# A two-layer hybrid decoder: attention units in the order diff, fox, diff, fox, each gate right behind its unit

## The chip, the cores and the metric

The kernel runs on one core of one Trainium2 chip. The metric is the device time of one execution in microseconds, taken as the median over several runs; the profile is of one such execution. A core has a matrix engine (TensorE, PE in the rows; its weight loads are the separate row PEld), VectorE (DVE), ScalarE (ACT), GpSimd (POOL) and SyncE (SP), which here only issues transfers. Each engine works through its own list of instructions in a fixed order and waits where an operand is not there yet.

## The reference

Two layers over 1040 tokens (16 meta tokens, 1024 of the sequence), width 1024. Each layer normalises h, multiplies it by one wide matrix `w_in`, and runs two kinds of attention on the parts: four **diff** heads (two softmaxes, the second subtracted with a weight, queries and keys turned by rope) and eight **fox** heads (one softmax each, with a running sum of forget gates added to the scores). Outputs are gated by silu(z), multiplied by `w_out` and added to h.

```
dq, dk, dv, dz, fq, fk, fv, fz, f_logit = split(u @ w_in)
p   = softmax(rope(q1) rope(k1)^T/8) - lam * softmax(rope(q2) rope(k2)^T/8)   # diff, causal
o_a = rms_norm(p @ dv, subln_g) * (1 - lambda_init)
cum = cumsum(log_sigmoid(f_logit + b_forget))
o_b = softmax(fq fk^T/8 + cum_q - cum_k) @ fv                                # fox, causal
h   = h + concat[o_a * silu(dz), o_b * silu(fz)] @ w_out
```

After the second layer comes a last RMSNorm; the meta tokens are dropped.

## The kernel before

A layer is cut into eight **units** of 128 columns: units 0 to 3 are the diff heads, units 4 to 7 hold two fox heads each. For a unit the kernel does

- `unit_proj`: k, q and v of the unit from `XTh`/`XTl` (the normalised input, transposed, as a rounded part and its rest). A product of fp32 quality is three matmuls: weights hi x input hi, weights lo x input hi, weights hi x input lo. One of k, q, v or z is 72 matmuls at L356. The weights come by DMA into `wraw` (SP) and are split on POOL into `whi` (L332) and `wlo` (L335). For diff units the key and query go through rope: the result is copied to `raw` (ACT), its halves are swapped by small transfers `sw<-raw` (SP), POOL multiplies by the sine table (L531), DVE by the cosine (L530) and adds (L532), and DVE makes the low parts (L538). Fox units have no rope.
- `attend`: scores into `pss` (L709 the high parts, L711 the low parts with the augmented rows), a masked minimum over them on DVE (L715) which also copies them to `E`, the exponential on ACT (L722), for diff one subtraction on DVE (L733), for fox a scaling on POOL (L739), transposes of `E` on PE (L884), their split by ACT (L792) and DVE (L793), and the products with V (L816 to L819).
- `sub_norm` for diff units and `unit_gate` (the z product and its multiplication into the output `OT`; the result goes to the DRAM buffers `ms`). With `from_dram` the gate first reads the ungated output back into `otl`.

`forget(l)` makes the running sum for the fox heads: the logits go out to the DRAM buffer `fx` and come back in another layout, ACT and DVE take the logarithm and a scan, one matmul with a triangular matrix (L483) carries sums across, and four small transfers write the results to the DRAM buffers `augq` and `augk`, from where each fox unit reads four rows into its low-part tiles `q2` and `k2` (the second operand of L711). `proj_v01` makes V of two units together with the forget logits, token by token.

In the loop of a layer, `unit_proj` of the next unit stands behind `attend` of the present one; in time the instructions of both are interleaved, because the builder's planner fixes each engine's order at build time. So while one unit's scores go through DVE, ACT and POOL, PE has the next unit's projection to do, and in the following a **step** means one unit's attention beside the next unit's projection. Before, a layer has three steps diff beside diff, one diff beside fox (unit 3), three fox beside fox and the last unit beside what is left. The gates of units 0, 1 and 2 stand behind their units, that of 3 behind unit 4, and those of 4 to 7 behind unit 7. After that come the transposed split of all gated outputs (L1088, L1089, from `mt<-ms`), and the product with `w_out` (L1109).

At the start, PE runs forty warm-up products (L970), then transposes the input, then projects k of unit 0. The four quarters of unit 0's k weights and of its q weights (`wroom`) are split on POOL.

## Time and profile before

| | |
|---|---|
| time, three runs | 1475.85 us median (1472.94 to 1477.03) |
| profiled execution | 1479.28 us; span in the trace 1477.5 us; mean granted clock 0.988 |
| PE busy / weight loads busy | 1425.7 us (96%) / 1353.0 us (92%) |
| DVE, ACT, POOL busy | 974.1, 696.1, 629.8 us (66%, 47%, 43%) |
| chain that ended last | PE 70%, DVE 5%, DMA 3%, ACT 2% of the span |

The table is read as follows: PE has work on hand nearly all the time, and the chain that ended last runs mostly through it; but its busy time counts pipelined matmuls by modelled ends, so the row of weight loads beside it, in which a stretch without work shows as a gap, is the stricter one. The other engines are busy half to two thirds of the span on average, and not evenly.

### The profile page before, as it was taken

Reading aid. Unit: us, or ns where it says so; the run is one execution under the profiler, and the core shown is the slowest. Engines: PE = TensorE matmul, PEld = TensorE weight load, DVE = VectorE, ACT = ScalarE, POOL = GpSimd, SP = SyncE. Lnnn points to the kernel's source line nnn. Section 1 sums busy time; section 2 is a strip of 40 time slices with the busy share of each in tenths; the row PEclk is TensorE's granted clock in tenths of the full one; section 3 lists DMA queues with packets and bytes.
Section 4 is the critical chain, followed back from the end, with each engine's and each line's share of the span. In section 5 each row is a group of like instructions: output and inputs, shape, how many; then the busy total and the mean of one; then the engine's idle time right before and its main releaser. Section 6 shows DMA issues by size and latency. Waiting matters only on the chain.

```text
span 1477.5 us, 26876 instructions
## 1 busy us (share of the span) xinstructions
PE 1425.7 (96%) x9302; PEld 1353.0 (92%) x9302; DVE 974.1 (66%) x2721; ACT 696.1 (47%) x1729; POOL 629.8 (43%) x1118
## 2 busy tenths in 40 slices
PE   6998989899999999999999999999999999999997
PEld 6997989799999999987889989899999999999886
DVE  6568776867665666574556587777867476755653
ACT  4336454445454555464223364545555365644511
POOL 4545454534244434555006345554424343445500
PEclk8999999999999999999999999999999999999999
DMA  8334321524043333465235142315322423244632
GB/s 195 75 52 63 56 64 33 76 25 98 23 88 63 63 68 43 120 206 105 86 118 126 27 62 49 71 44 72 57 51 64 90 38 80 62 98 105 221 114 86
DMA packets 112280, 119.64 MB, mean 81 GB/s; under 512 B 15440, under 2 KB 92880, under 8 KB 112144
## 3 DMA queue, kind: packets, MB, share of 16 engines
q1 hardware_dynamic: 106768, 105.14, 33.3%
q10 hardware_dynamic: 5376, 12.78, 3.5%
q8 instruction: 73, 1.20, 0.3%
q14 instruction: 63, 0.52, 0.1%
HBM read 70.92 MB, written 21.54 MB: 63 GB/s over the span
## 4 chain that ended last, share of the span: by engine, by line
PE 70%; DVE 5%; DMA 3%; ACT 2%; issue 1%; SPq 1%; POOL 1%; DVEq 0%; ACTq 0%
PE pj L356 33%; PE pss L1109 6%; PE pj L1109 5%; PE pt L884 3%; PE pss L709 3%; PE pss L711 3%; PE po L819 2%; PE po L818 2%; PE pj L436 2%; PE pt L1109 2%; DVE E L715 1%; SPq L144 1%; DMA wraw<-in_w_in_dram 1%; PE po L816 1%; DMA mt<-ms 1%
## 5 line engine op out<-in xcount | busy, mean ns | idle before, releaser
L356 PE MATMUL pj<-XTh,whi 128*128 128x346 f32 (+5 forms) x1392 | 452.6, 328 | 5.6 <-POOL whi L332 3.6
L356 PE MATMUL pj<-XTh,wlo 128*128 128x346 f32 (+5 forms) x1392 | 451.5, 325 | 5.9 <-POOL wlo L335 5.9
L356 PE MATMUL pj<-XTl,whi 128*128 128x346 f32 (+5 forms) x1392 | 451.3, 325 | 0.0
L356 PEld LDWEIGHTS pj<-XTh,whi 128*128 128x128 f32 x1392 | 262.8, 190 | 9.9 <-POOL whi L332 5.1
L356 PEld LDWEIGHTS pj<-XTh,wlo 128*128 128x128 f32 x1392 | 263.9, 190 | 7.7 <-POOL wlo L335 6.6
L715 DVE CUSTOM_DVE_ANT_0 E<-pss,cst 128x456 f32<-128x456 f32 (+6 forms) x384 | 211.8, 557 | 79.8 <-PE pss L711 61.9
L356 PEld LDWEIGHTS pj<-XTl,whi 128*128 128x128 f32 x1392 | 263.5, 190 | 0.9
L722 ACT ACTIVATE E<-E,cst 128x400 f32<-128x400 f32 (+2 forms) x192 | 172.4, 898 | 138.7 <-DVE cst L715 125.8
L335 POOL TENSOR_TENSOR wlo<-wraw,whi 128x256 fp32r<-128x256 f32 x232 | 181.8, 784 | 22.5 <-PE pj L356 7.6
L793 DVE TENSOR_TENSOR ptl<-pt,pth 128x512 fp32r<-128x512 f32 (+1 forms) x240 | 147.7, 633 | 41.5 <-ACT pth L792 36.4
L739 POOL TENSOR_SCALAR E<-E,cst 128x400 f32<-128x400 f32 (+2 forms) x96 | 84.5, 881 | 187.3 <-DVE cst L738 157.9
L709 PE MATMUL pss<-k,qa 128*128 128x400 f32 (+7 forms) x448 | 154.1, 347 | 9.3 <-DVE cst L715 7.2
L332 POOL TENSOR_SCALAR whi<-wraw 128x256 fp32r<-128x256 f32 x232 | 106.9, 461 | 110.6 <-DMA wraw<-in_w_in_dram 85.4
L792 ACT CAST pth<-pt 128x512 fp32r<-128x512 f32 (+1 forms) x240 | 123.7, 545 | 63.4 <-PE pt L900 29.7
L692 POOL TENSOR_SCALAR XTl<-ql 64x128 fp32r<-64x128 f32 x136 | 54.3, 401 | 185.2 <-PE pss L711 137.3
L709 PEld LDWEIGHTS pss<-k,qa 128*128 128x128 f32 x448 | 85.4, 191 | 17.5 <-DVE cst L715 14.0
L884 PE MATMUL pt<-cst,E 128*128 128x128 f32 x576 | 86.7, 274 | 4.2 <-DVE cst L715 2.9
L818 PE MATMUL po<-pth,V 128*128 128x256 f32 x320 | 84.2, 286 | 0.0
L819 PE MATMUL po<-ptl,V 128*128 128x256 f32 x320 | 83.1, 288 | 0.7 <-DVE ptl L793 0.5
L531 POOL TENSOR_TENSOR sw<-sw,sin 128x694 f32<-128x694 f32 (+5 forms) x32 | 53.2, 1666 | 55.5 <-DMA sw<-raw 42.8
L884 PEld LDWEIGHTS pt<-cst,E 128*128 128x128 f32 x576 | 68.0, 141 | 7.5 <-DVE cst L715 4.2
L711 PE MATMUL pss<-k,q 68*128 68x400 f32 (+6 forms) x224 | 72.2, 325 | 0.0
(301 smaller groups left out, 2971.0 us busy)
## 6 DMA issues: line engine op xcount, KB each, us to landing
wraw<-in_w_in_dram SPq DMA_DIRECT2D x248, 128.0 KB
hb<-in_x_dram SPq DMA_DIRECT2D x16, 512.0 KB
wor<-in_w_out_dram SPq DMA_DIRECT2D x64, 128.0 KB
ms<-OT SPq DMA_DIRECT2D x8, 520.0 KB
k<-k ACTq DMA_DIRECT2D x16, 260.0 KB
h<-hb SPq DMA_DIRECT2D x8, 512.0 KB
ms<-OT SPq DMA_DIRECT2D x8, 512.0 KB
hb<-h SPq DMA_DIRECT2D x8, 512.0 KB
```

The costliest lines, as they stand in the source:

```text
L335: nc.gpsimd.tensor_tensor(out=lo, in0=raw, in1=hi.bitcast(F32), op=ALU.subtract)
L356: nc.tensor.matmul(ps[:, :n], lhsT=w, rhs=xx[:, k, t0:t0 + n], start=(k == 0 and i == 0), stop=(k == KT - 1 and i == 2))
L709: nc.tensor.matmul(ps[:, :nn], lhsT=U.Qa[m][:, t:t + P], rhs=U.K1[m][:, c0:c0 + nn], start=True, stop=False)
L711: nc.tensor.matmul(ps[:, :nn], lhsT=low[m], rhs=U.Kb[m][:, c0:c0 + nn], start=False, stop=True)
L715: nc.vector.tensor_tensor_reduce(out=E[:, c0:c0 + n], in0=ps[:, :n], in1=k, scale=-1.0, scalar=s[:, c - 1:c] if CHN and c else -NEG, op0=A ...
L722: nc.scalar.activation(E[:, :W], E[:, :W], AF.Exp, scale=-1.0, bias=lo, accum_out=s[:, 4:5])
L792: nc.scalar.copy(hi, ps)
L793: nc.vector.tensor_tensor(out=lo, in0=ps, in1=hi.bitcast(F32), op=ALU.subtract)
L818: nc.tensor.matmul(o[:, :256], lhsT=U.V[:, kb, hd, :], rhs=hi, start=False, stop=False)
L819: nc.tensor.matmul(o[:, :256], lhsT=U.V[:, kb, hd, :], rhs=lo, start=False, stop=last)
L884: nc.tensor.transpose(ps[:, (2 * a + b) * P:(2 * a + b + 1) * P], PP[:, k0:k0 + P], ident)
L1109: nc.tensor.matmul(ps, lhsT=xx[:, k, m0:m0 + P], rhs=wo[k][w][:, c], start=(k == 0 and i == 0), stop=(k == KT - 1 and i == 2))
```

## The change

The units are taken in the order 0, 4, 1, 5, 2, 6, 3, 7, and every gate stands right behind its own unit, so that no gate reads its unit back from DRAM. Steps are then diff beside fox (four in a layer) and fox beside diff (three), and the last unit is again 7. Since unit 4 is now second, `forget(l)` is drained before its projection is, and `proj_v01` makes V of units 0 and 4. The rope tables get a tag of their own (two buffers; they shared the slots of `q2`), the buffers `ptl` go from four to three, unit 0's q weights are issued behind the k weights on POOL as well as on SP, and the warm-up has thirty products.

```diff
+ORD = (0, 4, 1, 5, 2, 6, 3, 7)
-PLB = 4
+PLB = 3
-WARM = 40
+WARM = 30
-Z_AT = {0: [0], 1: [1], 2: [2], 4: [3], 7: [4, 5, 6, 7]}
+Z_AT = {0: [0], 1: [1], 2: [2], 3: [3], 4: [4], 5: [5], 6: [6], 7: [7]}
...
-                col = unit_cols(u)[2]
+                col = unit_cols(ORD[u])[2]
...
-            for u in range(2):
-                x = ps[:, P * u:P * u + P]
-                nc.scalar.copy(Vs[u][:, b, 0, :], x)
-                nc.vector.tensor_tensor(out=Vs[u][:, b, 1, :], in0=x, in1=Vs[u][:, b, 0, :].bitcast(F32), op=ALU.subtract)
+            x = ps[:, 0:P]
+            nc.scalar.copy(Vs[0][:, b, 0, :], x)
+            nc.vector.tensor_tensor(out=Vs[0][:, b, 1, :], in0=x, in1=Vs[0][:, b, 0, :].bitcast(F32), op=ALU.subtract)
+            V, x = heads(Vs[1][:, b], "p a (c d) -> p (a c) d"), ps[:, P:2 * P].rearrange("p (m d) -> p m d", d=64)
+            nc.scalar.activation(V[:, 0::3, :], x, AF.Copy, scale=0.5)
+            nc.vector.scalar_tensor_tensor(out=V[:, 1:3, :], in0=x, scalar=0.5, in1=V[:, 0::3, :].bitcast(F32),
+                                           op0=ALU.mult, op1=ALU.subtract)
...
-    with tc.issue_after(last_of(SP)):
+    with tc.issue_after(last_of(SP)), tc.issue_after(last_of(POOL)):
         prefetch(0, "q")
     for l in range(DEPTH):
-        tabs = (q2t("cos", F32), q2t("sin", F32))
+        tabs = [big.tile([P, L], F32, name=nm, tag="tab", bufs=2) for nm in ("cos", "sin")]
...
-        for j in range(8):
+        for at, j in enumerate(ORD):
             run_late()
             drain(attend(units[j]))
             here = Z_AT.get(j, [])
-            if j < 7:
+            if j == 0:
+                drain(forget(l))
+            if at < 7:
                 if j >= 4 and j not in here:
                     dma(ms[j][:, tq:], units[j].OT[:, tq:])
-                drain(unit_proj(l, j + 1, units[j + 1], tabs))
-            if j == 0:
-                drain(forget(l))
+                drain(unit_proj(l, ORD[at + 1], units[ORD[at + 1]], tabs))
```

Line numbers of the changed kernel are higher by 2 near the top and by 13 to 15 from `proj_v01` on (L356 is L358 there, L483 L498, L711 L726).

The first place is PE around the triangular matmul of `forget` in layer 0. Before, scores of unit 1, a diff unit, follow it, which read neither `augq` nor `augk`:

```order
L779 MATMUL pt_1405<-XTl_97,sq_1402 128x1 x2
L483 MATMUL pt_1694<-cst_87 128x1
L709 MATMUL pss_1909<-k1_1410,qa1_1538 128x264
L711 MATMUL pss_1909<-k1_1410,XTl_97 128x264
L709 MATMUL pss_1968<-k0_1409,qa0_1537 128x256
```

Now, the low part of unit 4's scores (`q2`, `k2`, which hold the augmented rows) stands four rows behind it, and unit 1's k products (`pj_0_640`) stand behind that:

```order
L794 MATMUL pt_1396<-XTl_97,sq_1393 128x1 x2
L498 MATMUL pt_1424<-cst_87 128x1
L954 MATMUL pt_1685<-cst_87 128x16
L954 MATMUL pt_1688<-cst_87 128x128 x4
L954 MATMUL pt_1694<-cst_87 128x128 x4
L845 MATMUL pss_1812<-k2_1547,q2_1556 128x16
L726 MATMUL pss_1848<-k2_1547,q2_1556 128x400
L358 MATMUL pj_0_640_2466<-XTh_96,whi_2381 128x346
```

So only nine small transposes are left between the matmul that makes the sums and the first matmul that needs them back from DRAM. (In layer 1 there are, besides eight of these, 25 projection products in that place.)

The second place is SP's queue at the same point of the changed kernel, where writes to `augq` and `augk`, the reads of them, the store of unit 0's gated output and weights of the next projection stand in one line:

```order
L328 DMA wraw_2508<-in_w_in_dram 128x2x128
L328 DMA wraw_2514<-in_w_in_dram 128x2x128
L146 DMA augq_109<-cst_87 128x65 x2
L146 DMA augk_110<-cst_87 128x65 x2
L146 DMA q2_1556<-augq_109 4x1040
L146 DMA q2_1557<-ql_1555 64x1040
L146 DMA k2_1547<-augk_110 4x1040
L146 DMA k2_1550<-augk_110 4x1040
L146 DMA q2_1557<-augq_109 4x1040
L146 DMA ms0_101<-OT_954 128x1040
L328 DMA wraw_2520<-in_w_in_dram 128x2x128
```

Before, the first read of `augq` stands some two dozen transfers behind its write. The third place is POOL at the start of layer 0: before, two and two of the q splits (`wroom`) stood between the last quarters of unit 0's k weights:

```order
L332 TENSOR_SCALAR whi_197<-wraw4_180 128x256
L332 TENSOR_SCALAR wroom_346<-cst_87 128x256 x2
L335 TENSOR_TENSOR wlo_195<-wraw4_180,whi_193 128x256
L332 TENSOR_SCALAR wroom_346<-cst_87 128x256 x2
L335 TENSOR_TENSOR wlo_199<-wraw4_180,whi_197 128x256
L335 TENSOR_TENSOR wroom_346<-cst_87,wroom_346 128x256 x4
```

and now all of k's are ahead of q's:

```order
L334 TENSOR_SCALAR whi_187<-wraw4_170 128x256
L337 TENSOR_TENSOR wlo_185<-wraw4_170,whi_183 128x256
L337 TENSOR_TENSOR wlo_189<-wraw4_170,whi_187 128x256
L334 TENSOR_SCALAR wroom_336<-cst_87 128x256 x4
L337 TENSOR_TENSOR wroom_336<-cst_87,wroom_336 128x256 x4
```

The last two `wlo` of k no longer have q splits ahead of them.

## Rows read from the trace of the kernel before

**Rows 1.** Page, first part: span, and busy time by engine.

```profile
span 1477.5 us, 26876 instructions
PE 1425.7 (96%) x9302; PEld 1353.0 (92%) x9302; DVE 974.1 (66%) x2721; ACT 696.1 (47%) x1729; POOL 629.8 (43%) x1118
```

**Rows 2.** Windows, first score of a unit to the next's: layer 0 units 0–6, layer 1.

```profile
core 0: us, PE busy (x) PEld busy (x) DVE busy (x) ACT busy (x) POOL busy (x), PEclk, DMA share, GB/s
...
86.00:153.00 67.00, 61.70 (x395) 57.74 (x395) 50.93 (x138) 34.27 (x87) 34.83 (x60) 1.00 0.37 51
153.00:226.00 73.00, 68.66 (x461) 66.08 (x459) 57.40 (x161) 35.67 (x91) 36.14 (x62) 0.98 0.33 61
226.00:312.00 86.00, 78.56 (x510) 74.08 (x511) 59.72 (x161) 38.81 (x101) 38.30 (x66) 0.96 0.35 54
312.00:374.00 62.00, 61.79 (x423) 60.52 (x423) 46.56 (x146) 31.36 (x85) 24.94 (x53) 1.00 0.33 63
374.00:461.00 87.00, 87.00 (x610) 85.56 (x609) 52.03 (x161) 42.93 (x110) 36.41 (x72) 1.00 0.28 63
461.00:531.00 70.00, 69.94 (x489) 69.01 (x488) 45.00 (x139) 37.67 (x95) 30.18 (x59) 1.00 0.31 57
531.00:605.00 74.00, 73.69 (x519) 72.01 (x519) 45.20 (x141) 39.76 (x99) 32.57 (x65) 1.00 0.39 67
...
825.00:885.00 60.00, 56.73 (x363) 54.57 (x362) 47.28 (x128) 33.20 (x80) 30.22 (x51) 0.94 0.39 55
885.00:967.00 82.00, 78.40 (x532) 75.30 (x531) 60.22 (x161) 38.03 (x94) 39.05 (x65) 1.00 0.28 54
967.00:1039.00 72.00, 71.04 (x482) 68.69 (x481) 56.02 (x148) 35.12 (x86) 37.26 (x64) 1.00 0.39 61
1039.00:1097.00 58.00, 58.00 (x406) 57.47 (x405) 43.69 (x124) 30.69 (x78) 23.98 (x52) 1.00 0.35 67
1097.00:1175.00 78.00, 77.50 (x546) 76.45 (x545) 47.52 (x143) 38.41 (x95) 31.16 (x62) 1.00 0.28 64
1175.00:1239.00 64.00, 64.00 (x456) 63.32 (x454) 42.02 (x124) 36.34 (x85) 32.22 (x64) 1.00 0.35 64
1239.00:1299.00 60.00, 59.59 (x422) 58.27 (x420) 40.67 (x123) 35.66 (x84) 24.62 (x50) 1.00 0.34 67
```

**Rows 3.** Windows of 10 us inside unit 1 and unit 2 of layer 0.

```profile
180.00:190.00 10.00, 8.25 (x54) 7.20 (x53) 9.94 (x28) 3.92 (x9) 7.61 (x13) 1.00 0.57 107
230.00:240.00 10.00, 10.00 (x75) 9.96 (x74) 5.34 (x14) 4.32 (x10) 1.65 (x4) 1.00 0.00 0
```

**Rows 4.** Chain that ended last: projection matmuls back to back (start, duration).

```profile
1371.33 9.09 PE pj L356 x58
```

**Rows 5.** Line L532: duration in ns, min/median/max, first and last start, forms.

```profile
L532 DVE TENSOR_TENSOR raw<-raw,sw x32: 496/846/1637, 49.3 to 1016.2; 128x694 f32<-128x694 f32 x9, 128x346 f32<-128x346 f32 x9, 128x684 f32<-128x684 f32 x4, 128x340 f32<-128x340 f32 x4
```

**Rows 6.** Triangular matmul of the forget sums, and the writes of its results (lines).

```profile
L483 PE MATMUL pt<-cst x4: 250/250/250, 174.9 to 899.1; 128*128 128x1 f32 x4
L144 SPq DMA_DIRECT2D augq<-cst x4: 338/414/1238, 176.6 to 901.6; - x4
L144 SPq DMA_DIRECT2D augk<-cst x4: 319/418/424, 177.6 to 903.6; - x4
```

**Rows 7.** Chain that ended last: shortest and longest small transfer in it.

```profile
265.27 3.78 DMA sw<-raw
992.62 1.89 DMA sw<-raw
```

**Rows 8.** Timeline of POOL at the start, and PE's wait (idle before, releaser).

```profile
30.89 2.49 POOL L332 TENSOR_SCALAR wroom<-cst 128x256 fp32r<-128x256 f32 x2 [1.90 <-DMA cst<-in_w_in_dram]
33.34 1.70 POOL L335 TENSOR_TENSOR wlo<-wraw,whi 128x256 fp32r<-128x256 f32 x1
35.10 0.60 PE L356 MATMUL pj<-XTh,wlo 128*128 128x272 f32 x1 [5.04 <-POOL wlo L335]
```

**Rows 9.** Groups by line in 605 to 690 us, the end of layer 0.

```profile
L1089 DVE TENSOR_TENSOR XTl<-mt,XTh 128x400 fp32r<-128x400 f32 (+1 forms) x14 | 10.0, 739 | 4.7 <-ACT XTh L1088 4.6
```

More of the change, by code (lines that the diff above doesn't have):

```diff
@@ L19 @@
 DVE = mybir.EngineType.DVE
+POOL = mybir.EngineType.Pool
 AF = mybir.ActivationFunctionType
@@ L401, in load_v01, with heads @@
         return his, los
+    def heads(ap, how):
+        return ap.rearrange(how, d=64)
     def proj_v01(l, his, los):
@@ L419, in proj_v01 @@
         nc.vector.tensor_tensor(out=vm, in0=ps[0:NM, :NV], in1=vm, op=ALU.add)
-        for u in range(2):
-            Vm, x = Vms[u][:, 0, :], vm[:, P * u:P * u + P]
-            nc.gpsimd.memset(Vm.bitcast(F32), 0.0)
-            nc.scalar.copy(Vm[0:NM], x)
-            nc.scalar.copy(Vm[64:64 + NM], x)
-            nc.vector.tensor_tensor(out=Vm[32:32 + NM], in0=x, in1=Vm[0:NM].bitcast(F32), op=ALU.subtract)
+        nc.gpsimd.memset(Vms[0].bitcast(F32), 0.0)
+        nc.gpsimd.memset(Vms[1].bitcast(F32), 0.0)
+        Vm, x = Vms[0][:, 0, :], vm[:, 0:P]
+        nc.scalar.copy(Vm[0:NM], x)
+        nc.scalar.copy(Vm[64:64 + NM], x)
+        nc.vector.tensor_tensor(out=Vm[32:32 + NM], in0=x, in1=Vm[0:NM].bitcast(F32), op=ALU.subtract)
+        Vm, x = heads(Vms[1], "p a (c d) -> p (a c) d"), vm[:, P:2 * P].rearrange("p (m d) -> p m d", d=64)
+        for r in (slice(0, NM), slice(32, 32 + NM)):
+            nc.scalar.activation(Vm[r, 0::3, :], x, AF.Copy, scale=0.5)
+            nc.vector.scalar_tensor_tensor(out=Vm[r, 1:3, :], in0=x, scalar=0.5, in1=Vm[r, 0::3, :].bitcast(F32),
+                                           op0=ALU.mult, op1=ALU.subtract)
         fn = slot("fn").rearrange("p (h b) -> p h b", h=8)
@@ L437, in proj_v01 @@
                                      start=(k == 0 and i == 0), stop=(k == KT - 1 and i == 2))
-            for u in range(2):
-                x = ps[:, P * u:P * u + P]
-                nc.scalar.copy(Vs[u][:, b, 0, :], x)
-                nc.vector.tensor_tensor(out=Vs[u][:, b, 1, :], in0=x, in1=Vs[u][:, b, 0, :].bitcast(F32), op=ALU.subtract)
+            x = ps[:, 0:P]
[4 more added lines that the diff above has]
+            nc.vector.scalar_tensor_tensor(out=V[:, 1:3, :], in0=x, scalar=0.5, in1=V[:, 0::3, :].bitcast(F32),
+                                           op0=ALU.mult, op1=ALU.subtract)
             nc.vector.tensor_tensor(out=fn[:, :, b], in0=ps[:, 2 * P:NV], in1=bfb[:, l], op=ALU.add)
@@ L601, in unit_proj @@
                 U.Kb.append(k2[0:68])
-        if j == 1:
+        if j == ORD[1]:
             U.V, U.Vm = vpre[l]
```

## Prediction

> **What bounds the kernel now.** The first part of the page says PE is busy 96% of the span and its weight loads 92% [rows 1]. That is close to the end: the arithmetic on PE is the same after the change (it only loses ten warm-up products), so all a new order can win is what PE still loses. To find where it loses, I cut the span at the first score matmul of each unit and read each stretch from the table of windows. Busy PE is a modelled figure and hides gaps, so I take as lost what the weight loads leave of a stretch, PEld against its length [rows 2].
>
> The reader should see three kinds of step. Diff beside diff, three in each layer, loses 67.0 - 57.7 = 9.3, 6.9 and 11.9 us in layer 0, and 5.4, 6.7 and 3.3 in layer 1: 43.5 us. Diff beside fox, one in each layer, loses 1.5 and 0.5. Fox beside fox, three in each, loses 1.4, 1.0 and 2.0, then 1.6, 0.7 and 1.7: 8.4 in all. The sum is 53.9 us, and four fifths of it lie in diff beside diff.
>
> Why there? In those stretches DVE is busy for 69 to 79% of the time, in fox beside fox for 60 to 68% [rows 2]. That share alone doesn't decide: diff beside fox stands at 75% as well and loses next to nothing. The windows of 10 us show what does. From 180 to 190, inside unit 1, DVE is busy for 9.94 of 10 and the weight loads for 7.20; from 230 to 240 DVE is at 5.34 and the loads at 9.96 [rows 3]. PE loses where DVE is full for some 10 us on end, because PE's scores wait for a bank that DVE has yet to reduce. What fills it so is a diff unit's own scores and subtraction together with the rope of the next diff unit. So the kernel is bound by PE, and by DVE in bursts of six steps.
>
> **The change, part by part.**
>
> *The order of steps.* After, each layer has four steps diff beside fox and three fox beside diff. For the first kind I take the rows there are: 4 x 1.5 + 4 x 0.5 = 8 us. The second kind isn't in this trace: a fox unit's scores, which go through POOL's scaling and not DVE's subtraction, beside a diff unit's rope. It is bounded by its two parents: fox beside fox, mean 1.5 in layer 0 and 1.3 in layer 1, and diff beside diff, mean 9.4 and 5.1. I take 3 and 1.5 a step, 13.5 for six, nearer to fox beside fox, because the burst has lost the diff attention's half, while the rope stays. Together 21.5 against 53.9: **-32.4**. The bounds of the second kind move this by -5 and +30.
>
> *The wait for the forget sums.* This one is new. Before, nothing near reads `augq`; in the changed order of PE, unit 4's low-part score stands behind the triangular matmul with nine small transposes between them in layer 0. After that matmul comes, by the times of before, 1.7 us until the first write is issued (174.9 to 176.6); the `augk` writes start at 177.6 and two of them take 0.4 each on the queue, so all four are out 3.5 us behind it [rows 6]. A write must land, then a read is issued (0.5) and must land, and PE is in order: nothing behind the score can start, unit 1's k products included. The nearest rows for a small transfer that something waits for are `sw<-raw` on the chain, 1.89 at the shortest and 3.78 at the longest [rows 7]. In layer 0, with 1.1 us for the transposes as cover: 3.5 + 1.89 + 0.5 + 1.89 - 1.1 = 6.7 to 10.5 us. In layer 1 the 25 products in between, at 9.09/58 = 0.157 us each [rows 4], cover 3.9 more: 2.8 to 6.6. I take the middle: 8.4 + 4.5, **+12.9**.
>
> The Trainium skill, in "DMA: Bandwidth & Descriptors", section "Anatomy of one DMA — SWDGE (gpsimd) path", fits a constant of some 2.0 us to each transfer and puts most of it to the receipt of the last write, longest where the target is HBM, as it is for `augq`. The page is on transfers issued another way; with 2.0 for both, an estimate from that page, layer 0 would wait 6.9 and layer 1 3.0, and the sum would be 3 us lower.
>
> *What piles up behind it.* While PE waits, unit 1's projection isn't begun, and part of its products stood ahead of the wait. Unit 4's scores then have fewer products beside them, so they load DVE more densely than other steps of their kind. Bounds: nothing (DVE has emptied its queue in the wait), or as dense as a diff beside diff step, 9.4 - 3 = 6.4 and 5.1 - 1.5 = 3.6. I take half, **+5**.
>
> *Gates and the ends of layers.* Before, the gates of 4 to 7 run at the end of a layer, so three z products more, 72 x 0.157 = 11.3 us each, stand beside unit 7's attention and the split of the gated outputs. After, only unit 7's gate is left there. The gates' work isn't gone, it fills other steps; what is left at the end is the DVE work: unit 7's scores and fourteen splits at L1089, 10.0 us [rows 9], on a stretch of PE that is 23 to 34 us shorter. Bounds: 0, if the splits of earlier units are spread ahead, and +10 in layer 0 if they all stand in PE's way. I take half, 5, in layer 0 and 2 in layer 1, where the first units' gates stand further back: **+7**. The read-back of four units for each layer falls away; it lay on POOL and SP and I give it nothing, since its place is covered by the same three gates' products.
>
> *Start.* PE waits 5.04 us at 35.10 for the last `wlo` of unit 0's k; POOL had done q's splits in between, with a wait of 1.90 for their data and 2.49 of work [rows 8]. With k's four quarters first, `wlo` can end 1.90 + 2.49 = 4.4 us earlier. The q splits come behind it, and V's behind those, so the delay may come back at the V product (lower bound 0), or PE may lose none of the 5.04 any more (upper). I take **-4**.
>
> *Costed at nothing.* Ten warm-up products fewer: they run while PE waits for the first input. V of unit 4 in two strided operations for each block on ACT and DVE: it replaces unit 4's own evacuation of the same elements. `ptl` three deep: DVE's split and PE's use of it are a few hundred ns apart in all rows that I read; where it bites, it is part of the end of layer 0.
>
> *Sum.* -32.4 + 12.9 + 5 + 7 - 4 = **-11.5 us**. The profiled execution took 1479.28, so it would be 1467.8; it lies 3.4 above the median of the runs shown, so that 1475.85 becomes **1464.4**, say 1465.
>
> **The rivals.**
>
> *Fox beside diff loses as much as diff beside diff (slower).* DVE's rope addition shares the time with POOL's scaling of E, which diff attention lacks; L532 takes 846 ns at the median and up to 1637 [rows 5], so it can be stretched to twice, and it is with another engine on the same tiles that one expects this. Six steps then lose 3 x 9.4 + 3 x 5.1 = 43.5 instead of 13.5: +30, **1494**. It ends on the slower side (over 1480.3) when the six lose more than 13.5 + 11.5 + 4.4 = 29.4 together, 4.9 a step. Against it: fox beside fox has the same scaling, and diff beside fox at 75% of DVE lost 1 us.
>
> *The wait and the ends eat the gain (no change).* If the forget wait is at its upper bound (+4.2), the piled-up step too (+5), and layer 0's end (+5): -11.5 + 14 = +2.7, **1478**. SP's queue speaks for it: behind the reads stand the store of unit 0's gated output, which must wait for the gate, and behind it two quarters of unit 1's q weights, so that projection may start late as well. Against it, each is a bound.
>
> *More comes back than I think.* Fox beside diff at its lower bound (-5), nothing piled up (-5), ends of layers free (-7): -28, **1447**.
>
> That the change does nothing is excluded, since three quarters of the steps get another partner.
>
> **How the numbers follow.** Three runs of this kernel lie 0.28% apart, so about 0.3%, 4.4 us, can be told from no change: 1471.4 to 1480.3 is the same. My forecast, 1465 with a range of its own of 1456 to 1474 (the forget wait, the start and the ends each at one of their bounds): 0.47, of which 0.07 falls above 1471.4. No change by the wait and the ends: 0.17, of which 0.05 is slower. Fox beside diff as bad as diff beside diff, in whole or for the greater part: 0.17, of which 0.02 remains the same. More comes back: 0.19. Faster 0.40 + 0.19 = 0.59, same 0.07 + 0.12 + 0.02 = 0.21, slower 0.05 + 0.15 = 0.20. The range for 8 in 10 leaves out about a tenth at either end: from 1448 to 1486.
>
> **What would show it.** In the windows of the changed trace: steps diff beside fox should lose at most 2 us, fox beside diff 1 to 4; PE should wait once for the forget rows behind L498, 7 to 10 us in layer 0 and 3 to 7 in layer 1, released by a transfer into `q2` or `k2`; the wait at 35 us should be gone or down to 1; DVE should be full from the last unit's scores to the splits in layer 0. The prediction is wrong if fox beside diff loses over 5 us a step, if the forget wait is over 12 or missing, or if the steps' loss moves to another engine, for instance POOL, which has the weights to split and E to scale in each fox beside diff step.

## The result, and the profile after

The changed kernel takes 1499.89 us (median of 4 runs, 1498.22 to 1503.87) against 1476.44 for the kernel before, run beside it: a ratio of 1.0163, with an interval of 1.0137 to 1.0190. It is slower by 1.6%; 1465 had been forecast, in a range up to 1486. The profiled execution is the longest of the four, 1503.87.

The first part of the page after the change, beside [rows 1]:

```profile
span 1502.2 us, 26738 instructions
PE 1433.0 (95%) x9282; PEld 1358.3 (90%) x9282; DVE 963.0 (64%) x2725; ACT 701.6 (47%) x1729; POOL 617.3 (41%) x1116
```

The span is 24.7 us longer. The weight loads leave 143.9 us of it empty where they left 124.5. PE did no more work than before (twenty matmul records fewer), but what it did took 5.3 us more of load time. That goes with a lower clock (a mean of 0.980 granted, 0.988 before), not with work.

The table of windows of the changed kernel has the start, the seven steps of layer 0 and its end, then the steps and the end of layer 1 (columns as in [rows 2]; units in the order 0, 4, 1, 5, 2, 6, 3):

```profile
0.00:73.00 73.00, 54.77 (x368) 53.42 (x368) 48.55 (x97) 31.16 (x65) 40.38 (x63) 0.90 0.74 145
73.00:150.00 77.00, 75.73 (x516) 74.43 (x517) 44.59 (x154) 34.75 (x91) 23.05 (x52) 0.98 0.34 43
150.00:231.00 81.00, 67.33 (x404) 60.71 (x403) 50.21 (x153) 38.14 (x94) 34.14 (x58) 0.87 0.24 47
231.00:303.00 72.00, 71.73 (x494) 70.43 (x491) 48.24 (x143) 36.00 (x95) 28.07 (x62) 1.00 0.35 64
303.00:381.00 78.00, 76.69 (x525) 74.42 (x525) 50.48 (x149) 37.00 (x92) 43.25 (x72) 1.00 0.31 51
381.00:455.00 74.00, 73.41 (x503) 72.14 (x503) 51.58 (x149) 38.93 (x100) 28.17 (x61) 1.00 0.43 71
455.00:533.00 78.00, 77.58 (x533) 75.12 (x532) 51.79 (x151) 39.20 (x96) 45.07 (x73) 1.00 0.23 45
533.00:607.00 74.00, 73.20 (x503) 71.88 (x503) 50.75 (x147) 36.74 (x98) 30.34 (x65) 1.00 0.36 72
607.00:700.00 93.00, 85.34 (x538) 77.73 (x537) 63.92 (x180) 56.34 (x145) 41.74 (x72) 0.96 0.42 107
...
826.00:896.00 70.00, 68.78 (x476) 68.01 (x477) 45.95 (x147) 35.57 (x91) 20.21 (x47) 0.98 0.32 48
896.00:964.00 68.00, 61.31 (x411) 58.48 (x411) 45.11 (x128) 33.17 (x76) 35.91 (x56) 0.97 0.28 54
964.00:1038.00 74.00, 72.18 (x495) 70.73 (x493) 50.34 (x143) 37.19 (x92) 28.64 (x62) 1.00 0.34 66
1038.00:1115.00 77.00, 76.29 (x532) 74.90 (x531) 52.00 (x138) 37.72 (x88) 44.22 (x73) 1.00 0.27 47
1115.00:1187.00 72.00, 71.11 (x492) 70.40 (x491) 48.65 (x136) 36.68 (x91) 26.17 (x58) 1.00 0.40 74
1187.00:1264.00 77.00, 76.74 (x538) 75.67 (x537) 51.20 (x140) 38.99 (x91) 46.10 (x74) 1.00 0.20 41
1264.00:1333.00 69.00, 69.00 (x476) 68.48 (x476) 46.59 (x134) 34.32 (x86) 26.79 (x57) 1.00 0.40 85
1333.00:1425.00 92.00, 88.16 (x553) 80.96 (x552) 61.18 (x167) 55.11 (x135) 37.62 (x65) 0.96 0.31 99
```

Read length minus PEld, as in the prediction. Twelve of the fourteen steps lose little: diff beside fox 2.6, 1.6, 1.9 and 2.1 us in layer 0, then 2.0, 3.3, 1.6 and 0.5; fox beside diff 3.6 and 2.9, then 2.1 and 1.3. The two others are the second step of each layer, 81 - 60.7 = 20.3 and 9.5 us, with 403 and 411 matmuls where the other steps have 476 to 538. Look at their count before the waits: they are short of products. (The count alone doesn't decide: before, steps with 423 and 405 matmuls lost 1.5 and 0.5 us [rows 2].)

To compare kernels whose stretches lie elsewhere, and to take in the clock, I use a second count: each matmul of a trace is priced at 0.456 us for 1000 columns and 0.109 at least (full rate), and a stretch loses its length less that sum. The prices are from the kernel before, where a matmul of 128 columns is followed by the next after 0.109 us in the median, one of 346 after 0.159 and one of 512 after 0.234. The last stretch is counted to the last matmul. The sum is 1380.7 us for the kernel before and 1378.5 after. What is lost, in us:

```
                 start  L0 steps  L0 steps  L0    L1 steps  L1 steps  L1    sum
                        1-2       3-7       end   1-2       3-7       end
before           21.2   16.2      19.2      9.7   14.1       7.6       1.0   89.1
changed          25.0   30.5      11.3     16.9   14.7       8.2       9.2  115.9
```

The difference, 26.8 us, is 24.7 of span and 2.2 of warm-up that isn't there. Of it 14.3 lie in the first two steps of layer 0, 15.4 in the two ends and 3.8 at the start; the later steps of layer 0 give back 7.9, and layer 1's steps hardly changed.

### The profile page after: what moved, and what is told of

Read it like the earlier page. It is cut to its first block, busy times and chain, and to the rows that moved or that the text cites. A ratio compares the mean times of both kernels' runs of the same rounds, so it can differ in the third digit from the quotient of the medians.

```text
span 1502.2 us, 26738 instructions
## 1 busy us (share of the span) xinstructions
PE 1433.0 (95%) x9282; PEld 1358.3 (90%) x9282; DVE 963.0 (64%) x2725; ACT 701.6 (47%) x1729; POOL 617.3 (41%) x1116
## 4 chain that ended last, share of the span: by engine, by line
PE 78%; DMA 7%; DVE 7%; issue 3%; ACT 2%; SPq 2%; POOL 2%; DVEq 0%; ACTq 0%; POOLq 0%
PE pj L358 39%; PE pss L1124 6%; PE pj L1124 5%; PE pss L724 4%; PE pss L726 4%; PE pt L899 3%; DMA wraw<-in_w_in_dram 3%; PE pj L448 2%; PE po L834 2%; PE po L833 2%; DMA sw<-raw 2%; SPq L146 2%; PE pt L1124 1%; PE po L831 1%; PE po L829 1%
## 5 line engine op out<-in xcount | busy, mean ns | idle before, releaser
L358 PE MATMUL pj<-XTh,whi 128*128 128x346 f32 (+5 forms) x1392 | 455.0, 328 | 7.8 <-DVE OT L803 3.3
L358 PE MATMUL pj<-XTh,wlo 128*128 128x346 f32 (+5 forms) x1392 | 450.8, 325 | 1.4 <-POOL wlo L337 1.4
L358 PE MATMUL pj<-XTl,whi 128*128 128x346 f32 (+5 forms) x1392 | 449.3, 324 | 0.0
L358 PEld LDWEIGHTS pj<-XTh,whi 128*128 128x128 f32 x1392 | 263.2, 189 | 12.6 <-DVE OT L803 4.3
L358 PEld LDWEIGHTS pj<-XTh,wlo 128*128 128x128 f32 x1392 | 263.5, 189 | 2.9 <-POOL wlo L337 2.2
L358 PEld LDWEIGHTS pj<-XTl,whi 128*128 128x128 f32 x1392 | 263.3, 189 | 0.6
L730 DVE CUSTOM_DVE_ANT_0 E<-pss,cst 128x328 f32<-128x328 f32 (+6 forms) x384 | 211.4, 558 | 62.1 <-PE pss L726 45.2
L334 POOL TENSOR_SCALAR whi<-wraw 128x256 fp32r<-128x256 f32 x232 | 103.5, 446 | 177.7 <-DMA wraw<-in_w_in_dram 106.0
L807 ACT CAST pth<-pt 128x512 fp32r<-128x512 f32 (+1 forms) x240 | 127.4, 543 | 86.5 <-PE pt L899 44.1
L724 PE MATMUL pss<-k,qa 128*128 128x272 f32 (+5 forms) x448 | 153.4, 347 | 6.2 <-DVE cst L730 2.5
L754 POOL TENSOR_SCALAR E<-E,cst 128x400 f32<-128x400 f32 (+2 forms) x96 | 91.2, 950 | 131.2 <-DVE cst L753 119.3
L724 PEld LDWEIGHTS pss<-k,qa 128*128 128x128 f32 x448 | 85.6, 191 | 11.8 <-DVE cst L730 6.3
L899 PE MATMUL pt<-cst,E 128*128 128x128 f32 x576 | 89.9, 276 | 4.1 <-DVE ptl L808 1.4
L707 POOL TENSOR_SCALAR XTl<-ql 64x128 fp32r<-64x128 f32 x136 | 45.0, 335 | 108.4 <-PE pss L726 90.5
L834 PE MATMUL po<-ptl,V 128*128 128x256 f32 x320 | 86.3, 296 | 2.7 <-DVE ptl L808 2.4
L833 PE MATMUL po<-pth,V 128*128 128x256 f32 x320 | 87.4, 294 | 0.9 <-ACT pth L807 0.9
L695 POOL TENSOR_TENSOR OT<-OT,cst 128x346 f32<-128x346 f32 (+3 forms) x48 | 42.0, 881 | 88.6 <-DVE cst L693 36.9
L726 PE MATMUL pss<-k,q 68*128 68x400 f32 (+6 forms) x224 | 72.5, 330 | 0.0
```

The lines of the kernel that those rows point to most:

```text
L358: nc.tensor.matmul(ps[:, :n], lhsT=w, rhs=xx[:, k, t0:t0 + n], start=(k == 0 and i == 0), stop=(k == KT - 1 and i == 2))
L724: nc.tensor.matmul(ps[:, :nn], lhsT=U.Qa[m][:, t:t + P], rhs=U.K1[m][:, c0:c0 + nn], start=True, stop=False)
L726: nc.tensor.matmul(ps[:, :nn], lhsT=low[m], rhs=U.Kb[m][:, c0:c0 + nn], start=False, stop=True)
L730: nc.vector.tensor_tensor_reduce(out=E[:, c0:c0 + n], in0=ps[:, :n], in1=k, scale=-1.0, scalar=s[:, c - 1:c] if CHN and c else -NEG, op0=A ...
L807: nc.scalar.copy(hi, ps)
L833: nc.tensor.matmul(o[:, :256], lhsT=U.V[:, kb, hd, :], rhs=hi, start=False, stop=False)
```

## The experiments

The table goes on with all kernels that were run (first the sum of full-rate work; 24.7 us of it are added by the edit in the last two):

```
               work    start  L0 1-2  L0 3-7  L0 end  L1 1-2  L1 3-7  L1 end   sum   median   ratio to before
no_wait        1378.5  16.4   19.8    12.4    19.1     8.5     8.2     5.9    90.4  1478.48  1.0036 [1.0014, 1.0058]
forget_first   1378.5  26.0   31.9    13.9    15.8    15.0     5.9     5.5   114.0  1500.66  1.0163 [1.0129, 1.0197]
hold           1378.5  27.2   27.0     9.5    22.3    14.1    13.7     2.4   116.2  1503.24  1.0186 [1.0157, 1.0214]
hold_ff        1378.5  23.8   31.0    10.0    15.9    14.2     6.5     4.6   106.0  1493.29  1.0123 [1.0086, 1.0160]
hold_ff_l1     1378.5  27.5   29.0     9.5    15.5    15.0     5.6     0.9   103.1  1491.46  1.0103 [1.0077, 1.0128]
fox_later      1378.5  24.9   16.7     8.2    15.8    15.0    10.3     7.6    98.4  1486.32  1.0087 [1.0056, 1.0118]
fl_gb          1378.5  24.4   15.0    13.9     7.9    17.1    11.8     0.7    90.7  1479.66  1.0029 [1.0009, 1.0049]
gates_end      1378.5  27.9   29.4    24.7    17.5    21.8     8.3     1.2   130.8  1521.51  1.0318 [1.0282, 1.0355]
l1_gates       1378.5  24.4   30.0    13.8    15.5    13.3    10.2     0.8   108.0  1495.51  1.0127 [1.0095, 1.0159]
g6_end         1378.5  26.5   29.4    10.9    16.4    10.5     7.4     2.1   103.3  1492.49  1.0121 [1.0090, 1.0153]
gates_own      1380.7  36.5   30.8    33.5    39.7    15.8    20.8    15.4   192.5  1579.40  1.0700 [1.0664, 1.0736]
start_undone   1380.7  34.6   33.1    25.4    25.2    20.8    11.5     9.9   160.6  1551.40  1.0514 [1.0470, 1.0558]
knobs_only     1378.5  25.3   17.7    16.1     5.1    16.6     8.1     0.7    89.6  1478.23  1.0025 [1.0009, 1.0042]
v_own_before   1405.4  33.3   18.1    14.6    16.4    12.9     8.5     1.3   105.1  1518.05  1.0279 [1.0262, 1.0296]
v_own_ff       1403.2  26.0   11.8     4.8    16.7     7.4    15.9     4.9    87.4  1500.88  1.0165 [1.0146, 1.0184]
```

How far a column can be trusted is seen in l1_gates: PE's matmuls stand in the order of the changed kernel up to 1125 us, and up to there the columns of the two differ by as much as 2.5 us. In g6_end the order is the same up to 544 us; for forget_first, no_wait, gates_end, start_undone and v_own_ff the planner drew a new one from 31 us on.

**The forget wait: no_wait, forget_first.** The chain of waits of the changed kernel shows it as forecast, in layer 0 (start, duration):

```profile
161.36 0.24 PE pt L498 x2
...
162.77 1.71 DMA augq<-cst
...
164.56 2.61 DMA q<-augq
167.16 2.14 issue
169.30 0.35 PE pss L845
```

From the triangular matmul to the first use of its result it is 8 us. The last 2.14, "issue" on the chain, are a wait too: by the trace's semaphore rows PE's queue stands until 169.25 for the first read of `augk` into `k2`, which was issued at 165.75 and landed at 169.21. And not all of the gap is put down to the forget rows; these are two of PE's waits between 150 and 232 us, and L954 are the nine small transposes, which wait for unit 0's norm on DVE:

```profile
PE pss L845 <- issue: 3.2, 1, 3.2
...
PE pt L954 <- DVE cst L257: 2.3, 1, 2.3
```

Two windows of that place show what followed:

```profile
160.00:170.00 10.00, 3.82 (x20) 3.22 (x19) 4.20 (x21) 1.89 (x6) 1.85 (x3) 0.57 0.22 47
170.00:180.00 10.00, 10.00 (x52) 10.00 (x51) 3.48 (x13) 1.94 (x7) 5.39 (x10) 0.74 0.45 107
```

PE is idle for most of the first, the granted clock stands at 0.57 and 0.74, and in the second 18 products start 0.29 us apart instead of 0.16, some 2.3 us more. The wait isn't of the chain's making: the scan (L496) was done at 136.7, and the planner put the triangular matmul at 161.2.

no_wait lets unit 4 read constant rows, written early; it leaves out unit 4's forget sums, so its result is another function:

```diff
+dma(k2[64:68], (augc if j == 4 else augk)[:, 2 * (j - 4) + m])
-dma(k2[64:68], augk[:, 2 * (j - 4) + m])
```

> The changed kernel with one edit: unit 4 reads constant rows, written to DRAM at the start, in place of the forget rows (so units 5 to 7 alone have the forget sums; unit 4's output is another function). The forget chain still runs, nobody waits for it in the second step. Changed kernel: 1499.9. Theory 1, the wait for the forget sums and what piles up behind it is most of the loss (26.8 us lost on PE in the second step of layer 0, 11.3 in that of layer 1, against some 3 and 1.5 in other steps of the kind): 20 to 33 us faster, 1467 to 1480. Theory 2, the wait is only its own 5.5 us and a lower clock behind it, and fox beside diff in this place is dense anyway: 6 to 10 us faster, 1490 to 1494.

Measured 1478.48: 21 us faster, in theory 1's range. But of the 25.5 us that it loses less, 8.6 lie at the start and 6.2 in the first steps of layer 1, where PE never waited for these rows; 10.7 lie in the first two steps of layer 0, which still lose 19.8. forget_first keeps the data and moves the chain:

```diff
             run_late()
+            if j == 0:
+                drain(forget(l))
             drain(attend(units[j]))
             here = Z_AT.get(j, [])
-            if j == 0:
-                drain(forget(l))
```

> The changed kernel with forget(l) drained ahead of the first unit's attention, so that its triangular matmul stands 190 rows of PE ahead of unit 4's first low-part score (4 before). In the changed kernel the scan was done at 136.7 us and the triangular matmul ran at 161.2, so that the wait was made by the order and not by the chain. Theory 1 (the late triangular matmul makes the wait, and the wait makes some 10 us in layer 0 and 2 to 4 in layer 1, as with the constant rows): 1475 to 1486, no wait for q<-augq. Theory 2 (the planner's order as a whole decides; any edit redraws some 5000 of 8862 PE rows and moves the time by tens of us): anything from 1475 to 1540, with the losses in steps that the edit doesn't touch.

Measured 1500.66, no gain. `augq` was written at 116.3 and read back at 118.7 and nothing waited for it, yet the first two steps lose 31.9. The gap is there all the same, as a wait and a window of forget_first show:

```profile
PE pt L954 <- DVE cst L257: 2.5, 1, 2.5
```

```profile
180.00:190.00 10.00, 8.65 (x36) 7.97 (x37) 2.82 (x8) 1.44 (x6) 3.25 (x8) 0.56 0.13 53
```

The same transposes wait for unit 0's norm, the clock falls as before, and from 177.2 to 188.8 us 7.9 are lost with no wait for a forget row. So the wait is real, but taking it away alone gives nothing back: another took its place. Theory 1 falls as far as it makes the forget rows the main cause.

**Products drawn ahead: hold, hold_ff.** In the changed kernel a part of unit 1's products stands in the first step, 73 us of work there and 54 in the second. The edit holds them behind unit 4's first scores:

```diff
+            ga = attend(units[j])
+            if at == 1:
+                for _ in range(2):
+                    next(ga)
+                mark = last_of(PE)
+            drain(ga)
...
+                    with tc.issue_after(mark):
+                        drain(unit_proj(l, ORD[at + 1], units[ORD[at + 1]], tabs))
```

> The changed kernel with unit 1's projection held, on PE, behind unit 4's first scores, in both layers, so that none of its 216 products is drawn ahead into the first step. In the changed kernel the first step had 73 us of PE work beside 45 of DVE, the second 54 beside 50 (with 26.8 us lost), in layer 1 67 beside 45 and 57 beside 46 (11.3 lost). Theory 1 (a step loses by how near DVE's work comes to PE's: 2 us under 0.7, 9 from 0.75 to 0.85, 19 above 0.9 over nine kernels): both steps come to 0.7 to 0.8, step one loses 4 to 8 more, step two 12 to 17 less; 6 to 12 us faster, 1488 to 1494. Theory 2 (the forget wait is what the second step loses): the products held behind the wait don't shorten it; same within 4 us or slower.

> As hold, and forget(l) drained ahead of the first unit's attention, so that neither the late triangular matmul nor the missing products stand in the second step. Theory 1 (both count): 12 to 20 us faster than the changed kernel, 1480 to 1488. Theory 2 (missing products don't count): as forget_first, 1497 to 1502.

Measured 1503.24, as theory 2 of hold has it, and 1493.29, between the two ranges of hold_ff. With hold the first two steps lose 27.0 in place of 30.5, and the end of layer 0 took it back; but only 4 us of work moved, to 69 and 59, so that hold says little. hold_ff does share the work evenly, 70 and 71 us where forget_first has 77 and 63, and its first two steps lose 31.0 in place of 31.9, though as a whole it is 7 us faster. So in that order how the products are shared between the two steps isn't what costs. Their sum is left, and it stayed the same, 140 us.

**What is missing: v_own_ff, v_own_before, fox_later.** `proj_v01` makes V of two units ahead of the first attention, so the first step has one group of 72 products fewer. The edit makes V of the second unit again by its own projection and leaves the other unused (the line reads `j == 1` in the kernel before):

```diff
-        if j == ORD[1]:
+        if j < 0:
             U.V, U.Vm = vpre[l]
```

> forget_first with the same edit: unit 4 makes its V by its own projection and the one made ahead is left unused; 22.6 us of products more. Theory 3: the first two steps, which lost 31.8 and 15.0 there, lose 16 to 24 and 7 to 10; 1500 to 1512 against 1500.7. Rival: 1520 to 1526.

> The kernel before with one edit: unit 1 makes its V by its own projection, as units 2 to 7 do, though the V made with the forget logits is still made (and left unused). That adds 72 products to the first step of each layer, 11.3 us each at 9.09/58 us a product, 22.6 in all, and some 2 us of DVE a layer. Theory 3 (the first two steps of a layer lose 14 to 17 us whatever the order because V of two units is made ahead of them and one group of products is missing there beside the same work of DVE): their loss falls by 6 to 10 in each layer, 1480 to 1488. Rival (they lose by something else, as a diff unit's rope): the loss stays, 1496 to 1502.

In the new order, with 24.7 us of work added, the time is 1500.88, as without it (1500.66). Windows of the first two steps of layer 0, of forget_first and then of v_own_ff:

```profile
71.00:158.00 87.00, 82.26 (x545) 78.85 (x545) 43.72 (x153) 33.52 (x90) 23.19 (x50) 0.97 0.34 50
158.00:244.00 86.00, 75.53 (x481) 69.05 (x480) 59.67 (x167) 44.42 (x109) 40.07 (x69) 0.92 0.24 42
```

```profile
71.00:148.00 77.00, 74.74 (x510) 73.09 (x511) 44.53 (x159) 35.35 (x95) 22.80 (x48) 0.97 0.38 56
148.00:231.00 83.00, 81.13 (x563) 78.45 (x562) 58.10 (x165) 44.17 (x108) 42.82 (x74) 0.98 0.27 43
```

1073 matmuls take 160 us where 1026 took 173. The first two steps lose 11.8 in place of 31.9, in layer 1 7.4 in place of 15.0. So in forget_first's order those steps have room for the products that were made elsewhere. That the missing group alone makes the loss is not shown: no_wait, in another order of the planner's, has the same group missing and loses 28.3 in these steps of both layers. In the order of before the rival holds in the steps: the first two of layer 0 lose 18.1 (16.2 before). The whole, 1518.05, lies beyond both ranges: it is 41 us slower, 25 of them the added work, 12 at the start and 7 at the end of layer 0. There the missing products don't make the loss; the prediction's reading, a diff unit's scores beside rope on DVE, still fits it, and was not tested by itself.

fox_later brings the first fox unit third, V of units 0 and 1 being made ahead as before the change:

```diff
-ORD = (0, 4, 1, 5, 2, 6, 3, 7)
+ORD = (0, 1, 4, 2, 5, 3, 6, 7)
```

> The changed kernel with the order 0, 1, 4, 2, 5, 3, 6, 7 and V of units 0 and 1 made with the forget logits, as before the change. The first fox unit comes one step later, with a whole step between the triangular matmul and the first use of its result. One step more is diff beside diff (9 us in layer 0, 5 in layer 1 before) in each layer, one less diff beside fox. Theory 1 (forget wait and its pile-up): the second step's loss goes from 38 to some 14 in both layers, 1475 to 1483. Theory 2 (steps are dense whatever the wait): 1492 or more.

Measured 1486.32, 14 us faster than the changed kernel and between the ranges of its two theories. Its first two steps lose 16.7, as in the kernel before, and its two fox beside diff steps of layer 0 lose 2.5 and 2.9, a diff beside fox that comes directly before the first of them 6.2.

**The ends: l1_gates, gates_end, g6_end, fl_gb, gates_own, hold_ff_l1.** l1_gates leaves layer 0's order as it is and puts two gates of layer 1 back to its end:

```diff
+Z_AT1 = {0: [0], 1: [1], 2: [2], 3: [3], 4: [4], 7: [5, 6, 7]}
...
-            here = Z_AT.get(j, [])
+            here = (Z_AT if l == 0 else Z_AT1).get(j, [])
```

> The changed kernel with the gates of units 5 and 6 at the end again in layer 1 alone; layer 0's PE order stays as it is. Theory A (the end of layer 1 lost 9.2 us because unit 7's attention had no z products beside it): the end loses 1 to 2, steps 5 and 6 of layer 1 lose 1 to 3 more; 5 to 8 us faster, 1492 to 1495. Theory B (redrawn order decides): no clear gain, losses move elsewhere in layer 1.

Measured 1495.51, and the end of layer 1 loses 0.8 in place of 9.2. The windows of that time, of the changed kernel and then of l1_gates (unit 7's first scores stand at 1333.0 and 1312.3):

```profile
1383.00:1393.00 10.00, 7.42 (x45) 5.29 (x42) 9.21 (x23) 7.06 (x15) 1.80 (x7) 1.00 0.62 198
1393.00:1403.00 10.00, 8.74 (x37) 7.54 (x36) 8.94 (x23) 8.32 (x20) 6.33 (x7) 0.66 0.38 121
```

```profile
1383.00:1393.00 10.00, 10.00 (x74) 9.97 (x74) 6.76 (x15) 6.48 (x17) 2.06 (x3) 1.00 0.28 86
1393.00:1403.00 10.00, 10.00 (x58) 8.84 (x58) 9.69 (x15) 7.63 (x17) 4.68 (x6) 1.00 0.95 292
```

DVE is nearly as busy as in the other, 16.5 of 20 us against 18.2, but PE has products beside it, and the clock stays at 1.00 where it fell to 0.66. Theory A holds for layer 1. The gain is 4.4 us by the medians, with no overlap between the four times of either kernel, and 7.7 by the spans of the profiled executions. The other kernels place the gates in both layers: gates_end those of 5 and 6 at the end, g6_end that of 6, fl_gb is fox_later with the gates as before the change, gates_own the order of before with each gate behind its unit and `ptl` three deep:

```diff
-Z_AT = {0: [0], 1: [1], 2: [2], 3: [3], 4: [4], 5: [5], 6: [6], 7: [7]}
+Z_AT = {0: [0], 1: [1], 2: [2], 3: [3], 4: [4], 7: [5, 6, 7]}           # gates_end
+Z_AT = {0: [0], 1: [1], 2: [2], 3: [3], 4: [4], 5: [5], 7: [6, 7]}      # g6_end
+Z_AT = {0: [0], 1: [1], 2: [2], 6: [3], 7: [4, 5, 6, 7]}                # fl_gb
```

> The changed kernel with the gates of units 5 and 6 at the end of each layer again (read back from DRAM), the others behind their unit. Theory A: the ends of the layers lose 16.9 and 9.2 us on PE (9.7 and 1.0 before) because unit 7's attention has no z products left beside it; two gates of 11.3 us each there take back 5 to 7 in each layer, and units 5 and 6, whose steps lose 1 to 4, lose 1 to 3 more: 6 to 10 us faster, 1490 to 1494. Theory B: the ends lose by the split of the gated outputs on DVE, which is unchanged, and steps 5 and 6 need their gates: same within 3 us or slower.

> The changed kernel with the gate of unit 6 alone at the end, in both layers. If one gate is enough beside the last unit: end of layer 1 from 9.2 to some 3 us, end of layer 0 from 16.9 to some 10, steps as in the changed kernel: 1486 to 1492. If the redrawn order decides: 1500 to 1530, with new losses in the first two steps and at the start.

> fox_later (order 0, 1, 4, 2, 5, 3, 6, 7) with the gates placed as before the change: 0, 1 and 2 behind their units, 3 behind unit 6, 4 to 7 behind unit 7. If the two causes found so far are each what they seem: steps lose some 7 us less than in the kernel before (as in fox_later), the ends 5 to 8 each again in place of 15.8 and 7.6, the start 4 more than before: 1468 to 1476. If what a gate is worth depends on the order of units (the end of layer 0 kept 17.5 in gates_end): 1480 to 1490.

> The kernel before with every gate right behind its own unit and ptl three deep (needed to fit), the order of units 0 to 7 unchanged. Theory A (the ends of the layers lose because the z products are gone from there): ends lose 6 to 8 us more in each layer, the middle gains nothing or little: 1482 to 1494. Theory B (ends lose for another reason, such as the last unit following a diff unit): same as before within 4 us.

In layer 1 the end loses 0.7 to 2.1 in every kernel with a second gate or more there (before, gates_end, g6_end, l1_gates, fl_gb, knobs_only, hold_ff_l1, v_own_before), and 2.4 to 15.4 in those with one. In layer 0 one or two more gates don't do: 16.4 and 17.5; with the gates as before, fl_gb loses 7.9 where fox_later loses 15.8, and gates_own loses 39.7 where the kernel before loses 9.7. But v_own_before has the gates as before and loses 16.4 there, so gates don't settle that end. g6_end, at 1492.49, met its forecast in layer 1 and missed it in layer 0; fl_gb, at 1479.66, lies between its two ranges. The forecasts of gates_end and gates_own were far off: 1521.51 and 1579.40. Their ends answer to theory A in part, but their starts and steps lose 22 and 59 us more than those of the kernels that they come from.

> As hold_ff, with the gates of units 5 and 6 at the end of layer 1. If the three causes add: 5 to 8 us faster than hold_ff, 1473 to 1482, no faster than the kernel before since start and end of layer 0 still lose some 11 us more than there.

Measured 1491.46 where 1473 to 1482 was expected. It is 2 us faster than hold_ff, less than can be told: the end of layer 1 falls from 4.6 to 0.9 as in l1_gates, but the start loses 3.7 more.

**The start and the small edits: start_undone, knobs_only.**

```diff
-WARM = 30
+WARM = 40
...
-    with tc.issue_after(last_of(SP)), tc.issue_after(last_of(POOL)):
+    with tc.issue_after(last_of(SP)):
         prefetch(0, "q")
```

> The changed kernel with the start of before: forty warm-up products, q weights of unit 0 split between the k weights on POOL. In the changed kernel the V products began 5.4 us earlier, and PE then stood 6.2 us before the first score of unit 0, whose q wasn't ready. Theory A: the gain was only moved to that wait, the time is the same within 3 us. Theory B: the early start costs (a wait and a lower clock behind it, 25.0 us lost until the first scores against 21.2): 3 to 6 us faster. Theory C: the earlier k does help: 3 to 5 us slower.

> The kernel before (order 0 to 7, gates as before, V of units 0 and 1) with the small edits of the change alone: thirty warm-up products, q weights behind the k weights on POOL, rope tables in a tag of their own, ptl three deep. Theory 1 (the small edits are worth what the start gains, at most 5 us): 1470 to 1477. Theory 2 (redrawn order): 1480 to 1520 with losses in the diff beside diff steps that these edits don't touch.

knobs_only, all the small edits in the order of before, takes 1478.23, 0.25% more: under the 0.3% that can be told, and no gain. Its start loses 25.3, as much as that of the changed kernel, so what the start loses more than before goes with the small edits, not with the order of units. start_undone takes 1551.40, 51 us more than the changed kernel, and none of its theories had that. Its two longest single waits of PE:

```profile
PE pt L295 <- DVE u L280: 10.0, 1, 10.0
PE pss L844 <- DMA qa<-qa: 9.9, 1, 9.9
```

Both lie at the start, which loses 9.6 us more. Another 35 are lost where the edit touches nothing: 14.1 in the later steps of layer 0, 8.3 in its end, 6.1 in the first steps of layer 1, and less elsewhere. PE's matmuls stand in the changed kernel's order only up to 31 us: the planner drew a new one from there on. What in that order costs so much wasn't settled.

## Why the prediction was wrong

**Twelve of fourteen steps: right in kind, a little low.** The diff beside fox steps were taken at 1.5 and 0.5 us and lose 2.0 and 1.8 on average, the fox beside diff steps behind the first were taken at 3 and 1.5 and lose 3.2 and 1.7: 25.4 us in all for 17. The rival that fox beside diff loses like diff beside diff, with POOL's scaling against the rope, didn't come; the time it gave, 1494, came near by another way. (The 846 ns of L532 in that rival are a median over all sizes [rows 5]; at 694 columns alone the addition takes 857 to 1637.)

**The step that failed: what the second step of a layer loses besides the wait.** The prediction let the kind of a step set its loss. It laid all six fox beside diff steps at 3 and 1.5 us and put the rest of the second step into the forget wait and half a pile-up, 3 + 8.4 + 3.2 = 14.6 in layer 0 and 1.5 + 4.5 + 1.8 = 7.8 in layer 1. That step lost 20.3 and 9.5 by the weight loads, and 26.8 and 11.3 by the second count. Of the 26.8, 9.4 lie in the gap and the slow products behind it, from 161.4 to 175.2 us; the other 17.4 stand against 6.2, so that the pile-up is over twice its upper bound of 6.4. In layer 1, where no forget wait came, it is 11.3 against 3.3.

What the runs show in its place is that the loss goes more with the place than with the pair. Two thirds of what diff beside diff lost before, 28.3 of 43.5 us [rows 2], stood in the first two steps of a layer, and the prediction read that as a property of the pair. By the second count those places lost 30.3 us before and 45.2 after, though no step there is diff beside diff any more. forget_first shows that the rest doesn't hang on the forget rows, and v_own_ff that products can fill it: with a group of 72 put back, the first two steps lose 19.2 us in place of the 46.9 of forget_first. Why the changed kernel loses more there than the one before, which has a group missing too, is not settled; no_wait loses less with that group missing, and the planner's order differs in each. So the part of the 32.4 that was to come from the first two steps never came; what came is mostly from unit 2's step of layer 0, which lost 11.9 before.

**The forget wait: nearly the right size, in one place of two.** 8.4 was taken for layer 0; PE stood still for 2.3 and 3.2 us between 161.6 and 169.3, with 2.2 us of transposes in between, and lost 2.3 more by the lower clock, which the prediction left out. In layer 1, where 4.5 was taken, the 25 products in between covered it and PE waited only 2.3 us for the norm of unit 0 (L954). The two transfers on the chain took 1.71 and 2.61 us, the read of `augk` that PE waited for last 3.5; 1.89 to 3.78 were the bounds. The Trainium skill, in "DMA: Bandwidth & Descriptors", section "Anatomy of one DMA — SWDGE (gpsimd) path", has a constant of 2.0 for each transfer that GpSimd issues; the mean of the two is near it, 2.16, though SP issued them. What the wait alone costs isn't shown: in forget_first, which is as slow, the norm's wait stands in its place.

**Ends of layers: +7 taken, +15.4 measured** (7.2 and 8.2 by the second count). Layer 1 was taken at 2 for want of a reason; l1_gates shows that its end needs the products of a second gate. For layer 0 the bound of 10 was right and half of it too little.

**The start: -4 taken, +1.6 measured** (3.8 by the second count, 2.2 of which are the warm-up products that are gone and took no time of their own). The mechanism was right as far as it went: the wait at 35 us is gone, and the products with V's weights began at 54.87 in place of 60.32. But then PE stood before the first scores, as this part of the chain of the changed kernel shows:

```profile
66.12 0.74 ACT qa L560
66.86 0.02 issue
66.88 5.78 DMA qa<-qa
72.66 0.14 issue
72.80 0.35 PE pss L844
```

Unit 0's queries, moved between partitions by transfers of which this one took 5.78 us, landed from 72.7 to 74.9 us, only some 3 us earlier than before (75.7 to 77.8). And the order had the first scores ahead of 120 of the 208 V products of layer 0, all of which stood ahead of them before and would have covered the wait. The bound "nothing gained" should have read "given back at the next thing that is late".

By the second count the errors add up. The steps, wait and pile-up included, were to change by -14.5 and changed by +7.6; of these 22.1 us, 14.4 lie in the first two steps of layer 0, 4.4 in those of layer 1 and 3.3 in the others. With 8.4 in the ends and 5.6 at the start that is 36.1, from -11.5 to +24.7; each is towards slower. Open remain, besides the first two steps, the end of layer 0 in the new order (two more gates didn't help it, fl_gb shows that four do with diff and fox otherwise arranged), and how far any of these sums would hold in another order of the planner's: kernels with the same work but for the warm-up took 1478 to 1579 us.

No kernel that was run beat the one before. The nearest with a new order of units, fl_gb, has diff and fox alternating from the third unit on and the gates of before, and stands at 1.0029.

## What to carry to other kernels

Before a loss is put down to the kind of work in a stretch, weigh the bottleneck's own work in it against what the other engines do beside it: the stretch that lost most here held 54 us of PE's work at full rate beside 50 of DVE's, where the next step held 71 beside 48, and part of its products had been made ahead. When a gate or a projection is moved, ask what it covered where it stood. And where a planner draws the whole order anew, one edit isn't one difference: compare by stretches, and trust most those whose order the edit left alone, as l1_gates did.

## What the runs showed of the hardware that was not expected

In the 10 us in which PE was busy for 3.8, its granted clock was 0.57 on average, in the next 0.74, and after the gap matmuls of 346 columns started 0.29 us apart for 5 us where they start 0.16 apart otherwise; that is nearly the ratio of its two levels, 1.2 and 2.4 GHz. The same fall, to 0.66, followed the gap at the end of layer 1. So a gap in which PE stood still for 5.5 us cost 9.4 by the second count. In forget_first the clock fell to 0.56 behind the norm's wait.
